# A SwiGLU block's last product: operands combined on chip, or made beforehand in DRAM

## The chip, the core and the metric

One core of one Trainium2 chip runs the whole program. The metric is the time of one execution on the device in microseconds. The kernel before takes 923.42 us, the median of 3 runs (923.11 to 923.51).

## What is computed

One layer on 1024 rows x 1024 channels in float32: a modulation from the conditioning vector, a pooling mixer (`multiscale_pool`), a residual with a layer norm, a SwiGLU with 2816 hidden channels, and a second residual with a layer norm.

```python
mod_x = s_c @ mod_w[i] + mod_b[i]
sh1, sc1, g1, sh2, sc2, g2 = jnp.split(mod_x[:, None, :], N_MOD, axis=-1)
hx = x * (1.0 + sc1) + sh1
ox, oc = pool_mixer(hx, hc, pool_w[j], pool_scale[j], not last)
x = layer_norm(ALPHA * x + g1 * ox, ln_g[i, 0], ln_b[i, 0])
h = x * (1.0 + sc2) + sh2
gt, up = jnp.split(h @ w_in, 2, axis=-1)
y = (jax.nn.silu(gt) * up) @ w_out
x = layer_norm(ALPHA * x + g2 * y, ln_g[i, 1], ln_b[i, 1])
```

## The kernel before

A float32 product is done as three: each operand is split into a high part in float32r (a cast, on ScalarE) and the low part (source less high part, on VectorE), and TensorE multiplies high by high, high by low and low by high. The splits of the last two parts go through `split`, lines 303 to 305.

**Opening** (to about 300 us). Loads, the modulation vectors, the pooling mixer, the first layer norm, the transposed rows `h`, and the first products of the SwiGLU. The order of its jobs is written out by hand (`ORDER_OF_ISSUE`), and `ENGINE_OF` says which engine does what. GpSimd has few jobs at first: line 548 adds two weighted tiles of mod_w, 363 and 368 fill the bands `ends` and `starts` for the pooling of the second half of the rows, 649 multiplies three row tiles by g1, and 701 and 704 fold weighted tiles of mod_w for the second modulation; a column product on TensorE (723) and small VectorE instructions (730 to 734) make gain and shift from these.

**Middle** (about 300 to 604 us). A loop over the tiles f of 128 hidden channels, 2 to 21. GpSimd makes sums of weights (1015 to 1024), ScalarE and VectorE split them (1035, 1041), TensorE does 60 matmuls a tile (1048), VectorE makes the activations a from the banks (1058 to 1080), and SP stores them to DRAM (`a_out`, 1083). The scheduler sets the order of issue here, each engine works in its own order.

**Last product** (about 604 us to the end). y = a @ ffn_w_out in Winograd's form: seven products, each over the 11 pairs of hidden tiles, of half the rows by half the channels. The operands are sums and differences of blocks. They are made on the way: each product has a class with `load`, `combine`, `parts` and `after`; loads bring blocks of a and of ffn_w_out, `combine` and `after` add and subtract them on VectorE and GpSimd (lines 1225, 1253, 1318), `parts` names what is split. `run_ahead` keeps loads, combinations and splits some steps before the matmuls of `sub_pass` (1377), which also carries the jobs of the residual (by_line, 1398; add_into, 1457) and of the last layer norm. Blocks of ffn_w_out are loaded again for each product that uses them.

All DMAs are issued by SP, in order. Each waits for the landing of the one issued eight before it.

Of the kernel before, what the change touches and what calls it, by code (L numbers as in the profile page):

```python
# [256 lines left out]
def trunk_kernel(ctx: ExitStack, tc: tile.TileContext, x, c, mod_w, mod_b, ln_g, ln_b, ffn_w_in, ffn_w_out,  # L257
# [172 lines left out]
    def pool_span(half, g, n):  # L430
        """Input tile n of a half for width g: its columns of the half's bank, cut to what is not zero, the operand."""
# [80 lines left out]
    def mod_col(j, key, first, last):  # L512
        """Partial sums of chunk j as a column, channels on the partitions."""
# [16 lines left out]
    def mod_row(j, *parts):  # L530
        """Chunk j on every partition, in two banks."""
# [47 lines left out]
    def pooled(half, p, h):  # L579
        """256 x 2 columns of the rows at place p of a half through pool_w."""  # L580
# [40 lines left out]
    def scale_bank(h):  # L621
        """pool_scale on every partition."""
# [83 lines left out]
    def mod2_whole(q):  # L706
        """SC2's sum over the partitions as well, on the tensor engine."""
# [73 lines left out]
    a_of = [dram.tile([P, 2, 2, HALF], F32, tag=f"a{pair}", name=f"ad{pair}", bufs=1) for pair in range(NF // 2)]  # L781
# [88 lines left out]
    def pooled_weighed(p):  # L870
        """The shift adds (row sums) x (shift @ pool_w) where the operator's rows do not sum to zero."""
# [730 lines left out]
```

## Time and profile before

| | |
|---|---|
| median of 3 runs | 923.42 us |
| span of the profiled execution | 922.6 us |
| TensorE busy | 780.4 us (85%) |
| VectorE busy | 705.6 us (76%) |
| GpSimd busy | 468.6 us (51%) |
| ScalarE busy | 295.5 us (32%) |
| DMA | 159.81 MB, 173 GB/s on average |

The runs are whole executions; the span is that of one profiled execution, from the first to the last instruction, and lies 0.8 us below the median. PE is TensorE, DVE VectorE, ACT ScalarE, POOL GpSimd, SP the engine that issues DMAs. Matmuls overlap, so busy time of TensorE is no measure of its pace; the number of matmuls in a stretch is.

### The profile page before, as it was taken

Reading aid. Unit: us, or ns where it says so; the run is one execution under the profiler, and the core shown is the slowest. Engines: PE = TensorE matmul, PEld = TensorE weight load, DVE = VectorE, ACT = ScalarE, POOL = GpSimd, SP = SyncE. Lnnn points to the kernel's source line nnn. Section 1 sums busy time; section 2 is a strip of 40 time slices with the busy share of each in tenths; the row PEclk is TensorE's granted clock in tenths of the full one; section 3 lists DMA queues with packets and bytes.
Section 4 is the critical chain, followed back from the end, with each engine's and each line's share of the span. In section 5 each row is a group of like instructions: output and inputs, shape, how many; then the busy total and the mean of one; then the engine's idle time right before and its main releaser. Section 6 shows DMA issues by size and latency. Waiting matters only on the chain. (4 is left out here: it accounts for less than half of the span.)

```text
span 922.6 us, 9749 instructions
## 1 busy us (share of the span) xinstructions
PE 780.4 (85%) x3370; PEld 625.6 (68%) x3370; DVE 705.6 (76%) x782; ACT 295.5 (32%) x506; POOL 468.6 (51%) x273
## 2 busy tenths in 40 slices
PE   6997677888989999997989999859787978888475
PEld 6986555666868888776867787748565855666354
DVE  3579999995371866476575765586999999999996
ACT  2447446723222221122122222224322423334502
POOL 3148668671422434233243543170857577687695
PEclk8699889999989999999889999979898999999787
DMA  8995184823438544554636353669564746610102
GB/s 315 380 358 181 43 254 139 316 91 114 160 120 267 170 127 117 180 160 139 201 106 192 98 155 131 189 250 333 212 207 171 254 146 206 216 45 1 69 23 91
DMA packets 112726, 159.81 MB, mean 173 GB/s; under 512 B 6715, under 2 KB 73987, under 8 KB 112678
## 3 DMA queue, kind: packets, MB, share of 16 engines
q1 hardware_dynamic: 112678, 159.20, 51.6%
q8 instruction: 26, 0.43, 0.2%
q14 instruction: 22, 0.18, 0.1%
HBM read 127.72 MB, written 31.46 MB: 173 GB/s over the span
## 5 line engine op out<-in xcount | busy, mean ns | idle before, releaser
L1377 PE MATMUL ps_x<-yop,yop 128*128 128x512 f32 (+1 forms) x693 | 174.1, 410 | 49.5 <-DVE yop L305 40.8
L1048 PE MATMUL ps_v<-t,ws 128*128 128x512 f32 x792 | 191.3, 399 | 11.4 <-ACT ws L1035 10.3
L1377 PEld LDWEIGHTS ps_x<-yop,yop 128*128 128x128 f32 x693 | 133.3, 203 | 90.0 <-DVE yop L305 53.8
L1048 PEld LDWEIGHTS ps_v<-t,ws 128*128 128x128 f32 x792 | 151.6, 193 | 48.0 <-ACT ws L1035 12.4
L816 PE MATMUL ps_gate<-h,wih 128*128 128x512 f32 x352 | 119.5, 422 | 13.7 <-DVE wih L798 6.5
L305 DVE TENSOR_TENSOR yop<-ya,yop 128x512 fp32r<-128x512 f32 x101 | 111.6, 1129 | 10.5 <-ACT yop L304 10.4
L1041 DVE TENSOR_TENSOR ws<-s,ws 128x512 fp32r<-128x512 f32 x64 | 54.0, 850 | 80.2 <-ACT ws L1035 79.4
L1015 POOL TENSOR_TENSOR s<-raw,raw 128x512 f32<-128x512 f32 x22 | 31.1, 1411 | 134.7 <-DMA raw<-in_ffn_w_in 87.9
L1398 POOL TENSOR_TENSOR yrow<-yrow,yline 128x1024 f32<-128x1024 f32 (+2 forms) x32 | 77.5, 2431 | 38.0 <-ACT yline L1395 16.1
L816 PEld LDWEIGHTS ps_gate<-h,wih 128*128 128x128 f32 x352 | 71.5, 205 | 31.3 <-ACT gk L827 4.8
L304 ACT CAST yop<-ya 128x512 fp32r<-128x512 f32 x101 | 59.3, 617 | 96.2 <-PE ps_x L1377 61.5
L1035 ACT CAST ws<-s 128x512 fp32r<-128x512 f32 x66 | 40.4, 619 | 149.3 <-DMA ad<-a 40.9
L816 PE MATMUL ps_gate<-h,wil 128*128 128x512 f32 x176 | 74.1, 421 | 8.8 <-DVE wil L803 8.7
L1048 PE MATMUL ps_v<-h,ws 128*128 128x512 f32 x264 | 65.9, 400 | 15.2 <-DVE upb L1063 15.2
L1048 PEld LDWEIGHTS ps_v<-h,ws 128*128 128x128 f32 x264 | 50.5, 193 | 27.6 <-DVE upb L1063 17.2
L1377 PE MATMUL ps_y<-yop,yop 128*128 128x512 f32 x264 | 63.8, 400 | 4.1 <-DVE yop L305 4.0
L1225 POOL TENSOR_TENSOR ya<-ya,ya 128x512 f32<-128x512 f32 x25 | 40.6, 1623 | 49.9 <-DMA yw<-in_ffn_w_out 25.1
L1048 PE MATMUL ps_v<-t,wu 128*128 128x512 f32 x264 | 63.4, 389 | 0.0
L1377 PEld LDWEIGHTS ps_y<-yop,yop 128*128 128x128 f32 x264 | 49.8, 191 | 17.9 <-DVE yop L305 7.6
L1048 PEld LDWEIGHTS ps_v<-t,wu 128*128 128x128 f32 x264 | 49.6, 188 | 10.3
L481 DVE SCALAR_TENSOR_TENSOR acc<-mw,s_col,acc 128x1024 f32<-128x1024 f32 (+1 forms) x30 | 43.5, 1462 | 14.4 <-DMA mw<-in_mod_w 14.0
L1024 POOL TENSOR_TENSOR s<-raw,s 128x512 f32<-128x512 f32 x22 | 32.8, 1492 | 37.5 <-DVE ws L1041 37.5
(202 smaller groups left out, 1306.7 us busy)
## 6 DMA issues: line engine op xcount, KB each, us to landing
raw<-in_ffn_w_in SPq DMA_DIRECT2D x88, 256.0 KB, 4.5
mw<-in_mod_w SPq DMA_DIRECT2D x32, 512.0 KB, 6.6
yw<-in_ffn_w_out SPq DMA_DIRECT2D x56, 256.0 KB, 4.2
wi<-in_ffn_w_in SPq DMA_DIRECT2D x22, 512.0 KB, 5.0
ad<-a SPq DMA_DIRECT2D x22, 512.0 KB, 3.5
ya<-ad SPq DMA_DIRECT2D x22, 512.0 KB, 6.8
m<-in_mod_w SPq DMA_DIRECT2D x16, 512.0 KB, 9.1
yline<-in_ffn_w_out SPq DMA_DIRECT2D x27, 256.0 KB, 3.2
```

What stands on the lines that cost most here:

```text
L304: nc.scalar.copy(hi, src)
L305: nc.vector.tensor_tensor(lo, src, hi.bitcast(F32), ALU.subtract)
L481: nc.vector.scalar_tensor_tensor(acc, w, s_col[:, k : k + 1], acc, ALU.mult, ALU.add)
L816: nc.tensor.matmul(ps, x, y, start=k == n == 0, stop=k % 4 == 3 and n == 2, skip_group_check=k > 3)
L1015: nc.gpsimd.tensor_tensor(s, up1, up2, ALU.add)
L1024: nc.gpsimd.tensor_tensor(s, tiles["raw", f, 1][:, 0], s, ALU.subtract)
L1035: nc.scalar.copy(t[:, 0], source(f, name))
L1041: engine(pick(f"vl.{name}_{f}", "DVE")).tensor_tensor(t[:, 1], source(f, name), t[:, 0].bitcast(F32), ALU.subtract)
L1048: nc.tensor.matmul(ps, x, y, start=fresh and first, stop=last, skip_group_check=not fresh)
L1225: e.tensor_tensor(dst, x, y, ALU.subtract)
L1377: nc.tensor.matmul(ps, s[:, x, r * P : (r + 1) * P], t[:, y, d], start=fresh and j == m == 0, stop=j == PAIRS - 1 and m == 2, skip_group_c ...
L1398: nc.gpsimd.tensor_tensor(res[i][:, s], res[i][:, s], lines[name][:, s], op)
```

## The change

Three things change.

The combinations of ffn_w_out are made once for all pairs, in DRAM, by nine transfers that GpSimd issues (`e_step`): four sums e0 to e3 of blocks, each 128 x 11 x 512. A transfer copies a block, copies a sum, or accumulates a block onto a sum. The loop calls one for each tile from 3 to 11.

The combinations of the activations are made by VectorE in `a_out`, at the second tile of each pair, with four instructions of 128x512; SP stores a11, a2, s12 and s43 for each pair. Signs move to the end: some products are now subtracted from the residual (`take_from`).

The last product then only loads two ready blocks for each step (`step_load`), splits both at once (`step_split`, 128x1024), and multiplies. Additions to the residual go from GpSimd to VectorE, the product with g2 in the last of the seven goes from its weights to its result, and the last norm of the first half of the rows goes from ScalarE and GpSimd to two VectorE instructions a tile.

```diff
+    a11_of, a2_of, s12_of, s43_of = pieces("a11", 1), pieces("a2", 2), pieces("s12", 2), pieces("s43", 2)
+    e_of = [dram.tile([P, NF // 2, HALF], F32, tag=f"e{n}", name=f"ed{n}", bufs=1) for n in range(1, 5)]
...
     def a_out(f):
-        nc.sync.dma_start(a_of[f // 2][:, :, f % 2], tiles["a", f])
+        j, a = f // 2, tiles["a", f]
+        if f % 2 == 0:
+            nc.sync.dma_start(a11_of[j][:, 0], a[:, 0])
+            return
+        nc.sync.dma_start(a2_of[j], a)
+        a21, s12, s43 = tiles["a", f - 1][:, 1], act_tile(f"s12_{j}"), act_tile(f"s43_{j}")
+        s1, s2 = s12[:, 0], s12[:, 1]
+        nc.vector.tensor_tensor(s1, a[:, 1], a21, ALU.subtract)
+        nc.vector.scalar_tensor_tensor(s2, s1, -1.0, tiles["a", f - 1][:, 0], ALU.mult, ALU.subtract)
+        nc.sync.dma_start(s12_of[j], s12)
+        for n in range(2):
+            nc.vector.scalar_tensor_tensor(s43[:, n], a[:, n], -1.0, s2, ALU.mult, ALU.subtract)
+        nc.sync.dma_start(s43_of[j], s43)
...
-    class Product1:
-        def load(j):
...
-    products = (Product1, Product2, Product6, Product5, Product3, Product7, Product4)
...
+    w_out = ffn_w_out.rearrange("(j r p) d -> p r j d", p=P, r=2)
...
+    E_STEPS = [(0, block(0, 1), False), (2, block(0, 1), False), (0, block(0, 0), True), (2, block(1, 1), True),
+               (1, 0, False), (3, 2, False), (1, block(1, 1), True), (3, block(0, 0), True), (3, block(1, 0), True)]
+
+    def e_step(n):
+        dst, src, add = E_STEPS[n]
+        src = e_of[src] if isinstance(src, int) else src
+        nc.gpsimd.dma_start(e_of[dst], src, **({"accum_op": ALU.add} if add else {}))
...
+    PARTS = ((lambda j: a11_of[j][:, 0], lambda j: w_out[:, 0, j, first]),
+             (lambda j: a2_of[j][:, 0], lambda j: w_out[:, 1, j, first]),
+             (lambda j: s12_of[j][:, 1], lambda j: e_of[1][:, j]),
+             (lambda j: s12_of[j][:, 0], lambda j: e_of[0][:, j]),
+             (lambda j: s43_of[j][:, 0], lambda j: w_out[:, 1, j, second]),
+             (lambda j: s43_of[j][:, 1], lambda j: e_of[2][:, j]),
+             (lambda j: a2_of[j][:, 1], lambda j: e_of[3][:, j]))
...
+    def step_load(n):
+        t = raw[n] = big(f"yraw{n}", F32, (P, 2, HALF))
+        for m, part in enumerate(PARTS[n // PAIRS]):
+            nc.sync.dma_start(t[:, m], part(n % PAIRS))
+
+    def step_split(n):
+        hi, lo = (big(f"y{q}{n}", F32R, (P, 2, HALF)) for q in ("hi", "lo"))
+        split(hi, lo, raw.pop(n))
...
+    LOADS, SPLITS = 7, 3
...
     def add_into(i, s, src):
-        nc.gpsimd.tensor_tensor(res[i][:, s], res[i][:, s], src, ALU.add)
+        z = res[i][:, s]
+        nc.vector.tensor_tensor(z, z, src, ALU.add)
...
+    E_AT = PLANNED + 1
...
+        if 0 <= f - E_AT < len(E_STEPS):
+            e_step(f - E_AT)
...
-            jobs.append((r / 2 + 5, lambda i=i: row_norm(i, whole)))
...
+            jobs.append((2 * r + 5, lambda i=i: row_centre(i, whole)))
+            jobs.append((2 * r + 6, lambda i=i: row_scale(i, whole)))
...
-            nc.vector.tensor_tensor(res[i][:, d], ps, res[i][:, d], ALU.add)
+            scaled(c[r][:, d], ps, d)
+            add_into(i, d, c[r][:, d])
```

What each engine is given, in order, shows where the nine transfers come to stand. First GpSimd's program from the fill of the accumulator `acc` on, before; `mw` are tiles of mod_w, `ox` the pooled rows, `g` is g1, `m` tiles of mod_w for the second modulation. In brackets is what a row waits for: DMAHW and DMASW are landings of transfers that SP and GpSimd issued.

```order
L486 MEMSET acc_161 128x1024
L548 TENSOR_TENSOR mw_1_178<-mw_1_178,mw_3_183 128x1024 [waits Activation_49]
L363 TENSOR_SCALAR ends<-consts 128x4x128 [waits DMAHW6_49,DMAHW7_49,DMAHW2_49,DVE_49]
L363 TENSOR_SCALAR ends<-consts 128x4x8 [waits DMAHW1_49]
L368 TENSOR_SCALAR starts<-consts 128x4x8
L368 TENSOR_SCALAR starts<-consts 128x4x120
L548 TENSOR_TENSOR mw_1_300<-mw_1_300,mw_3_278 128x1024 [waits DMAHW2_49,Activation_49]
L649 TENSOR_TENSOR ox_2_456<-ox_2_456,g_89 128x1024 [waits DVE_49]
L649 TENSOR_TENSOR ox_1_415<-ox_1_415,g_89 128x1024
L649 TENSOR_TENSOR ox_0_417<-ox_0_417,g_89 128x1024 [waits Pool_49]
L701 TENSOR_TENSOR m_3_0_0_493<-m_3_0_0_493 128x512 [waits DMAHW7_49,Activation_49]
L701 TENSOR_TENSOR m_3_0_0_493<-m_3_0_0_493 128x256 [waits Pool_49]
```

The same engine in the changed kernel, from the second transfer on (the first stands five rows before). `ed_136` to `ed_139` are the sums e0 to e3; the line numbers of after are some lines further on.

```order
L1200 DMA ed_138<-in_ffn_w_out 1408x1x512
L1200 DMA ed_136<-in_ffn_w_out 1408x1x512 [waits DMASW0_49]
L548 TENSOR_TENSOR mw_1_215<-mw_1_215,mw_3_220 128x1024 [waits Activation_49]
L363 TENSOR_SCALAR ends<-consts 128x4x128 [waits DMAHW6_49,DMAHW7_49,DMAHW2_49,DVE_49]
L1200 DMA ed_138<-in_ffn_w_out 1408x1x512 [waits DMASW1_49]
L1200 DMA ed_137<-ed_136 64x11264 [waits DMASW2_49]
L363 TENSOR_SCALAR ends<-consts 128x4x8 [waits DMAHW1_49]
L368 TENSOR_SCALAR starts<-consts 128x4x8
L368 TENSOR_SCALAR starts<-consts 128x4x120
L1200 DMA ed_139<-ed_138 64x11264 [waits DMASW3_49]
```

All nine stand in the opening, though the loop calls them. Between the jobs of the first modulation stand a copy out of ffn_w_out, two accumulations that wait for the copies, and two copies of sums that wait for the accumulations. GpSimd goes on after them so:

```order
L548 TENSOR_TENSOR mw_1_337<-mw_1_337,mw_3_315 128x1024 [waits DMAHW2_49,Activation_49]
L1200 DMA ed_137<-in_ffn_w_out 1408x1x512 [waits DMASW4_49]
L1200 DMA ed_139<-in_ffn_w_out 1408x1x512 [waits DMASW5_49]
L649 TENSOR_TENSOR ox_2_493<-ox_2_493,g_89 128x1024 [waits DVE_49]
L649 TENSOR_TENSOR ox_1_452<-ox_1_452,g_89 128x1024
L649 TENSOR_TENSOR ox_0_454<-ox_0_454,g_89 128x1024 [waits Pool_49]
L701 TENSOR_TENSOR m_3_0_0_530<-m_3_0_0_530 128x512 [waits DMAHW7_49,Activation_49]
L1200 DMA ed_139<-in_ffn_w_out 1408x1x512 [waits DMASW7_49]
L701 TENSOR_TENSOR m_3_0_0_530<-m_3_0_0_530 128x256 [waits Pool_49]
```

The last accumulation stands between the first and the second fold and waits for the one before it. On VectorE, in the fourth of the seven products, before (`ya`, `yw`, `yline` are blocks, `yop` operands):

```order
L1225 TENSOR_TENSOR ya_4209<-ya_4209 128x512
L305 TENSOR_TENSOR yop_4223<-ya_4219,yop_4223 128x512 [waits PE_49,Activation_49]
L305 TENSOR_TENSOR yop_4224<-ya_4212,yop_4224 128x512 [waits Activation_49]
L1225 TENSOR_TENSOR ya_4210<-ya_4210 128x512
L305 TENSOR_TENSOR yop_4225<-ya_4220,yop_4225 128x512 [waits PE_49,Activation_49]
L305 TENSOR_TENSOR yop_4226<-yline_4239,yop_4226 128x512 [waits Activation_49]
```

And in the changed kernel, in the same product:

```order
L305 TENSOR_TENSOR ylo_5246<-yraw_5156,yhi_5245 128x1024 [waits DMAHW6_49,DMAHW5_49,Activation_49]
L305 TENSOR_TENSOR ylo_5265<-yraw_5177,yhi_5264 128x1024 [waits DMAHW7_49,DMAHW0_49,Activation_49]
L305 TENSOR_TENSOR ylo_5284<-yraw_5198,yhi_5283 128x1024 [waits DMAHW2_49,DMAHW1_49,Activation_49]
L305 TENSOR_TENSOR ylo_5303<-yraw_5219,yhi_5302 128x1024 [waits DMAHW4_49,DMAHW3_49,Activation_49]
L305 TENSOR_TENSOR ylo_5322<-yraw_5242,yhi_5321 128x1024 [waits DMAHW7_49,DMAHW0_49,Activation_49]
```

A step there is one instruction of 1024 in the place of three of 512.

## Rows read from the trace of the kernel before

**Rows 1.** The page: busy tenths of each engine, and of the DMA engines, in 40 equal slices of the span.

```profile
PE   6997677888989999997989999859787978888475
DVE  3579999995371866476575765586999999999996
POOL 3148668671422434233243543170857577687695
DMA  8995184823438544554636353669564746610102
```

**Rows 2.** Instructions that write or read the operands `yop` of the last product: line, engine, operation, count: shortest, median and longest in ns, start of the first and of the last in us.

```profile
L1377 PE MATMUL ps_x<-yop,yop x693: 277/389/796, 621.5 to 912.2; 128*128 128x512 f32 x158, 128*128 128x256 f32 x16
L305 DVE TENSOR_TENSOR yop<-ya,yop x101: 646/685/2904, 588.8 to 895.7; 128x512 fp32r<-128x512 f32 x101
```

**Rows 3.** Stretches of the trace: from and to in us, length, busy us of PE, PEld, DVE, ACT and POOL with their instructions, granted TensorE clock, DMA share, GB/s.

```profile
360.00:400.00 40.00, 39.84 (x175) 32.38 (x174) 22.63 (x31) 6.54 (x11) 12.30 (x9) 1.00 0.49 156
...
620.00:640.00 20.00, 20.00 (x90) 16.58 (x89) 14.71 (x19) 7.38 (x13) 3.30 (x2) 1.00 0.75 268
...
720.00:740.00 20.00, 19.71 (x87) 15.68 (x85) 20.00 (x22) 8.01 (x14) 11.43 (x7) 1.00 0.80 260
740.00:760.00 20.00, 14.24 (x57) 10.43 (x58) 20.00 (x23) 5.55 (x10) 15.24 (x11) 1.00 0.43 144
...
800.00:820.00 20.00, 15.37 (x55) 11.25 (x56) 20.00 (x18) 4.59 (x9) 15.47 (x10) 0.91 0.33 107
...
912.40:922.60 10.20, 0.07 (x1) 0.00 (x0) 6.58 (x13) 1.68 (x3) 4.58 (x5) 0.63 0.34 129
```

**Rows 4.** Groups of instructions from 660 us to the end: busy us, mean ns of one, idle time before them and what ended it.

```profile
L1377 PE MATMUL ps_x<-yop,yop 128*128 128x512 f32 x489 | 133.3, 428 | 35.8 <-DVE yop L305 35.7
L305 DVE TENSOR_TENSOR yop<-ya,yop 128x512 fp32r<-128x512 f32 x88 | 96.8, 1128 | 0.0
L1225 POOL TENSOR_TENSOR ya<-ya,ya 128x512 f32<-128x512 f32 x23 | 37.3, 1620 | 26.8 <-ACT yop L304 11.9 <-DVE ya L1225 7.5 <-DMA yw<-in_ffn_w_out 3.8
L1377 PE MATMUL ps_x<-yop,yop 128*128 128x256 f32 x66 | 9.5, 291 | 8.6 <-DVE yv L1551 8.6
```

**Rows 5.** Stretches of the opening, columns as in rows 3.

```profile
0.00:10.00 10.00, 8.77 (x49) 8.43 (x49) 0.31 (x2) 1.28 (x1) 1.63 (x8) 1.00 0.75 245
10.00:20.00 10.00, 4.12 (x18) 4.15 (x18) 4.96 (x5) 3.88 (x5) 2.31 (x1) 0.69 1.00 371
20.00:30.00 10.00, 8.28 (x45) 7.56 (x44) 6.25 (x9) 1.71 (x4) 4.96 (x5) 0.67 1.05 357
30.00:40.00 10.00, 10.00 (x41) 9.14 (x41) 6.24 (x12) 5.80 (x12) 0.00 (x0) 0.50 1.02 406
40.00:50.00 10.00, 10.00 (x81) 10.00 (x81) 8.06 (x10) 4.90 (x9) 2.40 (x1) 0.94 1.08 358
50.00:60.00 10.00, 10.00 (x49) 6.84 (x48) 5.32 (x7) 5.44 (x12) 1.67 (x1) 0.83 1.09 348
60.00:70.00 10.00, 10.00 (x73) 8.95 (x73) 9.86 (x12) 4.16 (x9) 10.00 (x4) 1.00 1.07 372
70.00:80.00 10.00, 5.69 (x36) 5.50 (x35) 9.89 (x12) 9.75 (x23) 9.69 (x8) 0.83 0.76 283
...
90.00:100.00 10.00, 6.36 (x48) 5.60 (x46) 9.65 (x20) 5.09 (x11) 6.20 (x6) 0.96 0.05 19
```

**Rows 6.** GpSimd in order of time: start and length in us, what it does, in brackets the idle time before and what ended it.

```profile
58.33 9.98 POOL L649 TENSOR_TENSOR ox<-ox,g 128x1024 f32<-128x1024 f32 x3 [13.79 <-DVE g L630]
68.27 6.72 POOL L701 TENSOR_TENSOR m<-m 128x512 f32<-128x512 f32 x4
75.07 0.73 POOL L704 TENSOR_TENSOR m<-m,m 128x256 f32<-128x256 f32 x1
```

**Rows 7.** VectorE in order of time, two rows: a residual sum that takes one of GpSimd's products by g1, and the first instruction on the columns of the second modulation.

```profile
62.91 3.18 DVE L654 SCALAR_TENSOR_TENSOR x<-x,ox 128x1024 f32<-128x1024 f32 x1
...
82.06 0.14 DVE L730 SCALAR_TENSOR_TENSOR sc<-ps_m,cols 128x2 f32<-128x2 f32 x1
```

**Rows 8.** Durations of single kinds: a 1024-wide addition on VectorE (order of time), a 1024-wide pass of ScalarE, and a 512-wide addition from a bank on VectorE (groups).

```profile
51.14 1.23 DVE L552 TENSOR_TENSOR acc<-acc,mw 128x1024 f32<-128x1024 f32 x1
...
L1395 ACT ACTIVATE yline<-yline 128x1024 f32<-128x1024 f32 x2 | 2.1, 1060 | 8.3 <-DMA yline<-in_ln_g 4.7 <-DMA yline<-in_ln_b 3.6
...
L1535 DVE TENSOR_TENSOR c<-ps_x,u 128x512 f32<-128x512 f32 x4 | 2.5, 676 | 0.0
```

**Rows 9.** The middle part: one stretch (columns as in rows 3), a wait in total (us, times, longest) from 300 to 600 us, and a group from 300 to 641 us.

```profile
300.00:604.00 304.00, 287.48 (x1226) 232.35 (x1225) 191.18 (x248) 70.22 (x118) 108.68 (x75) 0.98 0.49 154
...
PE ps_v L1048 <- ACT ws L1035: 10.3, 5, 4.5
...
L1063 DVE TENSOR_TENSOR upb<-ps_v,upb 128x512 f32<-128x512 f32 x21 | 14.5, 688 | 0.5
```

**Rows 10.** DMA issues: what they move, queue, count, KB of one, median us from issue to landing.

```profile
yw<-in_ffn_w_out SPq DMA_DIRECT2D x56, 256.0 KB, 4.2
ad<-a SPq DMA_DIRECT2D x22, 512.0 KB, 3.5
ya<-ad SPq DMA_DIRECT2D x22, 512.0 KB, 6.8
...
out<-yrow SPq DMA_DIRECT2D x5, 256.0 KB, 2.0
```

More of the change, by code (lines that the diff above doesn't have):

```diff
@@ L779, in spill, with pieces @@
                 for pair in range(NF // 2)]
-    a_of = [dram.tile([P, 2, 2, HALF], F32, tag=f"a{pair}", name=f"ad{pair}", bufs=1) for pair in range(NF // 2)]
+    def pieces(name, count):
+        return [dram.tile([P, count, HALF], F32, tag=f"{name}{pair}", name=f"{name}d{pair}", bufs=1)
+                for pair in range(NF // 2)]
+    a11_of, a2_of, s12_of, s43_of = pieces("a11", 1), pieces("a2", 2), pieces("s12", 2), pieces("s43", 2)
+    e_of = [dram.tile([P, NF // 2, HALF], F32, tag=f"e{n}", name=f"ed{n}", bufs=1) for n in range(1, 5)]
     p1_of, gate_of = spill("p"), spill("g")
@@ L1199, in trunk_kernel @@
-    borrowed, closed = set(), set()
-    def lend(hs, back=False):
-        if back:
-            closed.update(map(id, hs))
-            w_free[:] = [h for h in w_free if id(h) not in closed]
-        else:
-            borrowed.update(map(id, hs))
-            w_free.extend(hs)
-    def w_release(h):
-        if id(h) not in closed:
-            w_free.append(h)
-    def hidden_load(half, j):
-        t = a_raw[half, j] = two(a_mem[half * PAIRS + j])
-        nc.sync.dma_start(t, a_of[j][:, half])
@@ L1218, in w_load @@
-    def w_load(key, j, rows, s):
-        t = raw[key, j] = w_free.pop(next(n for n, h in enumerate(w_free) if key != "d" or id(h) not in borrowed))
-        f = 2 * j + rows
-        nc.sync.dma_start(t, ffn_w_out[f * P : (f + 1) * P, s])
-    def less(e, dst, x, y):
-        e.tensor_tensor(dst, x, y, ALU.subtract)
-    def weight(key, j):
-        t = raw.pop((key, j))
-        spent.append(t)
-        return t
-    spent = []
-    class Product1:
-        def load(j):
-            hidden_load(0, j)
-            w_load("b11", j, 0, first)
-        def combine(j):
-            pass
-        def parts(j):
-            return a_raw[0, j][:, 0], weight("b11", j)
@@ L1307, in trunk_kernel @@
-    class Product7:
-        def load(j):
-            pass
-        def combine(j):
-            pass
-        def parts(j):
-            return a_raw[0, j][:, 0], a_raw[0, j][:, 1]
-        def after(j):
-            nc.gpsimd.tensor_tensor(raw["d", j], raw["d", j], g2[:, first], ALU.mult)
-            op_free.append(two(place("big", y_place[f"ya{j}"], f"yop{OPS + j}", F32R, (P, 1024))))
-    class Product4:
-        def load(j):
-            pass
-        def combine(j):
-            pass
-        def parts(j):
-            return a_raw[1, j][:, 1], weight("d", j)
@@ L1331, in trunk_kernel @@
-    products = (Product1, Product2, Product6, Product5, Product3, Product7, Product4)
-    steps = [(q, j) for q in range(7) for j in range(PAIRS)]
-    done = {"load": 0, "combine": 0, "parts": 0}
-    def split_parts(q, j):
-        pair = []
-        for n, src in enumerate(products[q].parts(j)):
-            t = op_free.pop(0)
-            split(t[:, 0], t[:, 1], src)
-            pair.append(t)
-        operands[q, j] = pair
-    def advance(kind, upto):
-        while done[kind] < min(upto, len(steps)):
-            q, j = steps[done[kind]]
-            if kind == "load" and len(w_free) < 4 and q > 1:
-                break
-            split_parts(q, j) if kind == "parts" else getattr(products[q], kind)(j)
-            if kind == "parts" and hasattr(products[q], "after"):
-                products[q].after(j)
-            while spent:
-                w_release(spent.pop(0))
+    w_out = ffn_w_out.rearrange("(j r p) d -> p r j d", p=P, r=2)
@@ new lines, in trunk_kernel @@
+    done = {"load": 0, "split": 0}
+    def step_load(n):
[5 more added lines that the diff above has]
+        split(hi, lo, raw.pop(n))
+        operands[n] = hi, lo
+        done_with("big", f"yraw{n}")
+    def advance(kind, upto):
+        while done[kind] < min(upto, STEPS):
+            {"load": step_load, "split": step_split}[kind](done[kind])
@@ L1353, in advance @@
             done[kind] += 1
+    LOADS, SPLITS = 7, 3
     def run_ahead(step):
         advance("load", step + LOADS)
-        advance("combine", step + COMBINES)
-        advance("parts", step + SPLITS)
-        while len(op_free) >= 8 and done["parts"] < min(step + 6, len(steps)):
-            advance("parts", done["parts"] + 1)
+        advance("split", step + SPLITS)
     def sub_pass(q, banks, fresh, heads, tails, jobs=()):
@@ L1507, in trunk_kernel @@
     second_products(NF - 1)
-    done_with("half", f"both{NF - 1}", f"upb{NF - 1}")
-    done_with("bank", f"ps_v{NF - 1}_5", f"ps_v{NF - 1}_7")
+    f = NF - 1
+    done_with("big", f"ws4_{f}", f"wu2_{f}", f"gate_{f // 2}", f"p1_{f // 2}", f"a_{f - 1}", f"a_{f}",
+              f"s12_{f // 2}", f"s43_{f // 2}")
+    done_with("big", *(name for name in LASTING["big"] if name[:2] in ("t4", "h1")))
+    done_with("half", f"both{f}", f"upb{f}")
+    done_with("bank", f"ps_v{f}_5", f"ps_v{f}_7")
     run_ahead(0)
@@ L1552, in trunk_kernel @@
         for r, i in enumerate(ORDER[1]):
-            for n, (s, src) in enumerate(((second, v[r]), (first, u[r]))):
+            for n, (s, src, into) in enumerate(((second, v[r], take_from), (first, u[r], add_into))):
                 more.append((r + n / 2, lambda s=s, src=src: scaled(src, src, s)))
-                more.append((r + n / 2 + 1, lambda i=i, s=s, src=src: add_into(i, s, src)))
+                more.append((r + n / 2 + 1, lambda i=i, s=s, src=src, into=into: into(i, s, src)))
             more.append((r + 3, lambda i=i: row_stats(i, 1, second)))
```

124 lines of the change are left out of this document (27 added, 97 removed).

## Prediction, before the changed kernel was run

> **What bounds the kernel now.** I read the page's slices first, then stretches of the last part, then groups and waits there, and last the opening, because the new transfers stand there in the order of issue. The slices show VectorE at nine tenths from slice 27 to the end, with TensorE below it, and the DMA engines full in the first three slices and never again [rows 1]. So two places count: the last product, and the opening.
>
> The last product runs from its first matmul at 621.5 us to the end at 922.6, so 301 us [rows 2]. TensorE at full pace issues 90 matmuls in 20 us, 0.222 us each, in the stretch from 620 on; from 740 and from 800 it issues 57 and 55 while VectorE is busy for all 20.00 us [rows 3]. VectorE bounds it, and TensorE's longest wait there is for VectorE's split [rows 4]. A split of 128x512 takes 1.13 us on average, though an undisturbed one takes 0.69 (the median), because GpSimd's combinations of 1.6 us each run beside it [rows 2, 4].
>
> In the opening the DMA share is 1.00 to 1.09 from 10 to 70 us, at 348 to 406 GB/s [rows 5]. GpSimd, idle for 13.79 us before it, starts the products by g1 at 58.33 as soon as VectorE has made g1, and VectorE's residual sums follow these [rows 6, 7].
>
> **Last product: the gain.** All combinations leave it (VectorE's and GpSimd's lines 1225 and 1253, GpSimd's 1318), and 154 splits of 512 become 77 of 1024. Nothing of it is left on GpSimd but the residual's lines. What remains:
> - TensorE: 891 matmuls of 512 x 0.222 = 198.0, and 66 half-width ones, 9.5 us busy [rows 3, 4]: 207.5 us.
> - VectorE: 77 splits x 1.23, the undisturbed 128x1024 subtraction or addition [rows 8], = 95 us. Evacuations, products with g2, additions now on VectorE, statistics: about 80 instructions of 0.68 [rows 8] = 54; eight 1024-wide norm steps x 1.23 = 10. Sum 159, below 207.5.
> - ScalarE: 77 casts x 1.06 [rows 8] = 82.
> - Loads: 154 of 256 KB = 40.4 MB in 207.5 us, 195 GB/s; 720 to 740 already moves 260 [rows 3].
>
> So TensorE becomes the bound. It won't be perfect: from 360 to 400 it issues 175 of a possible 180 [rows 3], so I put 207.5 / 0.972 = 213.5. Add 7 us for the starts of seven products (1 us each, an estimate: one bank's evacuation of 0.68 and a handoff [rows 8]), the tail of 10.2 us after the last matmul [rows 3] and 0.7 for the extra product with g2 in it: 231. Gain 301 - 231 = **70 us**. Bounds: 76 at full pace, 50 if TensorE keeps only the pace of the middle part, 1226 x 0.222 = 272 of 304 us [rows 9].
>
> **Middle part: four more VectorE instructions for each pair.** 11 x 4 x 0.69 [rows 9] = 30 us on VectorE, which is busy for 191 of 304 us. They stand ahead of the next tiles' splits, as the order shows, and behind those waits ScalarE, GpSimd's next sum and TensorE. TensorE waits for a split or cast at 5 of the 20 tiles now [rows 9], so I take a quarter: **8 us**; bounds 0 and 30. The two further stores to a pair on SP's queue hold back the loads behind them by the same instructions, and are in these bounds.
>
> **The nine DRAM transfers: the loss.** The loop calls them at tiles 3 to 11, but they read only a kernel input, and the order of issue puts them at the head of GpSimd's program. Call them A to I in that order: A, B copies out of ffn_w_out, C, D accumulations, E, F copies of one sum into another, G, H, I accumulations; each writes 1408 x 512 x 4 = 2.88 MB. C waits for A, D for B, E for C, F for D, G for E, H for F, I for H. GpSimd is in order, so behind E's wait stand the bands `ends` and `starts`, behind F's the sum for g1, behind H's three products by g1, and behind I's wait, which is H's landing, all folds of the second modulation.
>
> Who waits for that: VectorE's residual sums wait for the products, and its columns at 82.06 need the first folds, which GpSimd did from 68.27 to 75.8 [rows 6, 7]. VectorE is in order too and is busy for 9.86 and 9.89 us of the two stretches from 60 to 80 [rows 5]. So the opening ends later by what delays the second fold, at 70.0 now, less some 3 us between the fold's columns and VectorE's arrival.
>
> The price of a transfer isn't in this trace, where nothing is copied from DRAM to DRAM or accumulated. The nearest row is a load under a full DMA: 357 GB/s [rows 5], 2.88 MB in 8.1 us. I take **8 us for a copy** and, as an accumulation must read its target as well, **16 us for an accumulation**. Below, 7.1 us for either (406 GB/s). Above, from 512 KB rows that include their latency [rows 10]: a store to DRAM 3.5 us, so 19 us for 2.88 MB, and a load from a spill 6.8 us, so 37 for an accumulation. The descriptor work on GpSimd I put at nothing: it lies beside the transfers it feeds; without that cover it is unpriced here, and the upper bound has to hold it.
>
> The Trainium skill (Collectives: The Full Stack, "The bandwidth ceiling: the fold count and why AG ≠ RS ≠ AR") says that an adding transfer runs at half a copy's rate because it needs two source reads; no run here shows it yet. The same skill (DMA: Bandwidth & Descriptors, "Latency and other measured facts") has copies between HBM tensors at about 207 GB/s, with longer rows than these; by that a copy is an estimated 14 us and an accumulation 28, and the kernel would take 1033 us.
>
> Until I can be issued, A to H must have landed: 4 x 8 + 4 x 16 = 96 us of all DMA engines. In the same time the opening's own loads up to 70 us must come, 70.6 us of all engines (the shares of the first seven stretches [rows 5]), and the engines are full, so the two add: 167. I add 6 us for three handoffs in which a chain's next transfer isn't yet moving, at 2.0 us, the shortest landing [rows 10]. GpSimd's second fold starts at 173 instead of 70; less 3: **100 us later**. Bounds: 8 x 7.1 + 70.6 - 73 = 54; and 4 x 19 + 4 x 37 + 70.6 - 73 = 222. Little of it comes back: from 90 to 100 the DMA is nearly idle, but VectorE is busy for 9.65 of 10 us [rows 5].
>
> **Sum**, against the profiled execution: 922.6 + 100 + 8 - 70 = 960.6. The runs' median, 923.42, is 0.8 above its span, so 961.4: **961 us, slower**.
>
> **Rivals.**
> 1. *The transfers pass beside the loads.* If the full share comes from the side of on-chip memory, a DRAM to DRAM transfer may not add to it. For it: the engines are idle around 95 [rows 5]. Then A to H, two chains of 8 to 16 us, land by about 75, the delay is 0 to 5, and the time 923.4 + 8 - 70 = 861. Against it: packets of a kind that already fill every engine's time.
> 2. *An accumulation costs no more than a copy.* 8 x 8 + 70.6 + 6 - 73 = 68, so 929; with both lower bounds (54, gain 76, middle 0) 901. This straddles the time before.
> 3. *Accumulations are dear, or their descriptors are*: up to 222 us, so 1083. For it: small pieces of 2 KB, and a wait before each. It shows as GpSimd held for over 200 us.
> 4. *The wait moves inside the last product*: TensorE then waits for loads instead of VectorE, and only half the gain is left, 996. Against it: eight loads are in flight and land in about 4 us [rows 10], seven steps are loaded ahead.
> That the change doesn't do what it says is in part certain: the loop doesn't spread the transfers.
>
> **Chances.** Forecast and what lies near it, with rival 4 (935 to 1000): 0.45. Rival 3 (over 1000): 0.25. Rival 2 (900 to 935): 0.17. Rival 1 (under 900): 0.13. The slow side decides once the delay of GpSimd exceeds 62 us. A range from 885 to 1060 leaves out about half of rival 1 and a third to a half of rival 3; the forecast's own is 935 to 1000. Faster by over 0.2% (about what a measurement can tell from no change): rival 1 and half of rival 2, 0.21; within 0.2%: 0.02; slower: 0.77.
>
> **What would show it.** GpSimd's second fold near 170; DMA share at 1 well past 100 us and more bytes written early; g1's products late by 50 to 80. In the last product, TensorE at 85 or more matmuls in 20 us, VectorE at 7 to 8 tenths, splits at 1.2 to 1.3 us. If the fold stands near 75, rival 1 holds and I am wrong on the sign; if near 140, rival 2.

## The result: half a per cent slower

The changed kernel takes 927.6 us (median of 6 runs, 925.17 to 928.83), the kernel before 923.26 us (6 runs, three of them timed beside it): a ratio of 1.005, interval 1.0034 to 1.0066. The sign was forecast, the size was not: +38 us predicted, about +4 measured.

The page of the changed kernel, busy tenths in 40 slices, answers to [rows 1]:

```profile
PE   4563565777788989899999999999659999999964
DVE  1232452899995381468678777788695764458987
POOL 2212235577662340334253426433445300000005
DMA  9999999974823437266476654746459857571612
```

The DMA engines stand at nine tenths for eight slices of 23 us, where before one stood at eight tenths and two at nine; VectorE stands at one to five tenths in the first six, and in most of the last ten TensorE is at nine tenths and VectorE below it. So both effects that the prediction named are there. Three places cut the time into parts: the last product for the gate on TensorE (the opening's end) in the kernel before, then in the changed one, and the first and last matmul of the changed kernel's last product, which answers to [rows 2]:

```profile
282.81 0.39 PE L816 MATMUL ps_gate<-h,wil 128*128 128x512 f32 x1
```

```profile
359.68 0.39 PE L823 MATMUL ps_gate<-h,wil 128*128 128x512 f32 x1
...
L1250 PE MATMUL ps_x<-yhi x231: 277/389/628, 690.6 to 912.9; 128*128 128x512 f32 x105, 128*128 128x256 f32 x11
```

| part | before, us | after, us | measured | forecast |
|---|---|---|---|---|
| opening, to the last product for the gate | 282.8 | 359.7 | +76.9 | +100 |
| middle, to the first matmul of the last product | 338.7 | 330.9 | -7.8 | +8 |
| last product, to the end of the span | 301.1 | 235.9 | -65.2 | -70 |
| span | 922.6 | 926.5 | +3.9 | +38 |

The opening is where the loss is. GpSimd in order of time (answers to [rows 6]); L1200 are the transfers, here C, D, E and F, and I in the row before the last:

```profile
18.89 1.76 POOL L1200 DMA_DIRECT2D ed<-in_ffn_w_out  x1 [13.98 <-DMA ed<-in_ffn_w_out]
33.96 1.80 POOL L1200 DMA_DIRECT2D ed<-in_ffn_w_out  x1
54.45 0.55 POOL L1200 DMA_DIRECT2D ed<-ed  x1 [18.69 <-DMA ed<-in_ffn_w_out]
80.11 0.56 POOL L1200 DMA_DIRECT2D ed<-ed  x1 [22.14 <-DMA ed<-in_ffn_w_out]
...
111.37 9.95 POOL L649 TENSOR_TENSOR ox<-ox,g 128x1024 f32<-128x1024 f32 x3 [11.77 <-DVE g L630]
...
137.77 2.03 POOL L1200 DMA_DIRECT2D ed<-in_ffn_w_out  x1 [14.94 <-DMA ed<-in_ffn_w_out]
138.67 3.91 POOL L701 TENSOR_TENSOR m<-m 128x256 f32<-128x256 f32 x3
```

The products by g1 come 53 us later than in [rows 6]. The second fold starts at 138.67; the prediction had it at 173. Below, what each queue of DMAs had done in the first 138 us: packets, MB, time of its packets as a share of 16 engines. q0 carries GpSimd's transfers, q1 what SP issues.

```profile
q0 software_dynamic: 7296, 23.07, 67.4%
q1 hardware_dynamic: 8516, 17.44, 37.6%
```

In 138 us the transfers A to H took 0.674 x 138 = 93 us of all engines; the prediction's price was 96. The loads took 52 us, and not the 70.6 that had been needed to get there in [rows 5]. That is the main difference, and it is taken up below. The engines stay full behind it (columns as in [rows 3]; the last three are clock, DMA share and GB/s):

```profile
80.00:110.00 30.00, 13.22 (x34) 8.46 (x35) 6.28 (x6) 3.32 (x6) 6.41 (x4) 0.56 1.02 290
...
140.00:180.00 40.00, 25.59 (x158) 23.16 (x157) 20.63 (x43) 20.12 (x43) 20.13 (x20) 0.77 1.09 310
```

Behind the fold it is the loads that come late. [rows 7] has VectorE's first columns of the second modulation at 82.06; now they come at 146.84, 65 us later. The next ones come at 172.36, 77 us later (95.52 before), since ScalarE waits for a load of mod_w in between:

```profile
163.57 0.51 ACT L696 ACTIVATE m<-m,s_col 128x256 f32<-128x256 f32 x1 [13.29 <-DMA m<-in_mod_w]
...
172.36 0.15 DVE L730 SCALAR_TENSOR_TENSOR sc<-ps_m,cols 128x2 f32<-128x2 f32 x1
```

In the last product TensorE is now the bound until about 870 us, and VectorE again near the end:

```profile
740.00:760.00 20.00, 20.00 (x90) 16.57 (x89) 11.48 (x14) 4.22 (x4) 0.00 (x0) 1.00 0.58 189
...
860.00:880.00 20.00, 20.00 (x98) 16.86 (x97) 20.00 (x23) 6.94 (x7) 0.00 (x0) 1.00 0.70 236
880.00:900.00 20.00, 12.81 (x44) 8.51 (x43) 18.69 (x26) 1.05 (x1) 0.00 (x0) 0.72 0.16 53
```

### The profile page after: what moved, and what is told of

Its sections match the earlier page's. It is cut to its first block, busy times and chain, and to the rows that moved or that the text cites. A ratio compares the mean times of both kernels' runs of the same rounds, so it can differ in the third digit from the quotient of the medians.

```text
span 926.5 us, 9471 instructions
## 1 busy us (share of the span) xinstructions
PE 770.6 (83%) x3370; PEld 631.3 (68%) x3370; DVE 612.0 (66%) x724; ACT 282.2 (30%) x425; POOL 314.9 (34%) x191
## 3 DMA queue, kind: packets, MB, share of 16 engines
q0 software_dynamic: 8720, 25.95, 11.7%
## 4 chain that ended last, share of the span: by engine, by line
PE 33%; DVE 26%; DMA 17%; issue 8%; SPq 8%; POOL 4%; ACT 2%; POOLq 0%; DVEq 0%; ACTq 0%
PE ps_v L1055 14%; PE ps_x L1250 14%; DMA mw<-in_mod_w 5%; SPq L332 5%; PE ps_y L1250 3%; DVE acc L481 3%; DMA m<-in_mod_w 3%; DVE ws L1048 3%; SPq L387 2%; PE ps_gate L823 2%; DMA halo<-in_x 2%; DVE wil L810 2%; DMA raw<-in_ffn_w_in 2%; DVE ylo L305 1%; DMA wi<-in_ffn_w_in 1%
## 5 line engine op out<-in xcount | busy, mean ns | idle before, releaser
L304 ACT CAST yhi<-yraw 128x1024 fp32r<-128x1024 f32 x77 | 78.1, 1050 | 118.0 <-DMA yraw<-in_ffn_w_out 38.1
L305 DVE TENSOR_TENSOR ylo<-yraw,yhi 128x1024 fp32r<-128x1024 f32 x77 | 99.2, 1327 | 13.5 <-ACT yhi L304 13.5
L1272 POOL TENSOR_TENSOR yrow<-yrow,line_lg 128x1024 f32<-128x1024 f32 (+2 forms) x12 | 26.7, 2229 | 222.5 <-ACT yrow L1303 183.2
L1250 PE MATMUL ps_x<-ylo,yhi 128*128 128x512 f32 (+1 forms) x231 | 90.0, 390 | 7.2 <-DVE ylo L305 7.0
L1250 PE MATMUL ps_x<-yhi 128*128 128x512 f32 (+1 forms) x231 | 89.0, 385 | 0.0
L1250 PE MATMUL ps_x<-yhi,ylo 128*128 128x512 f32 (+1 forms) x231 | 89.0, 385 | 0.0
L1048 DVE TENSOR_TENSOR ws<-s,ws 128x512 fp32r<-128x512 f32 x64 | 58.0, 910 | 43.6 <-ACT ws L1042 42.7
L1027 POOL TENSOR_TENSOR s<-s,raw 128x512 f32<-128x512 f32 x22 | 33.0, 1501 | 86.8 <-DVE ws L1048 86.7
L1250 PEld LDWEIGHTS ps_x<-ylo,yhi 128*128 128x128 f32 x231 | 44.3, 192 | 18.5 <-DVE ylo L305 10.2
L1250 PEld LDWEIGHTS ps_x<-yhi 128*128 128x128 f32 x231 | 44.3, 192 | 8.6
```

The source lines that it names most:

```text
L304: nc.scalar.copy(hi, src)
L305: nc.vector.tensor_tensor(lo, src, hi.bitcast(F32), ALU.subtract)
L1027: nc.gpsimd.tensor_tensor(s, s, tiles["raw", f, 0][:, 0], ALU.subtract)
L1048: engine(pick(f"vl.{name}_{f}", "DVE")).tensor_tensor(t[:, 1], source(f, name), t[:, 0].bitcast(F32), ALU.subtract)
L1250: nc.tensor.matmul(ps, s[x][:, r * P : (r + 1) * P], t[y][:, d], start=fresh and j == m == 0, stop=j == PAIRS - 1 and m == 2, skip_group_c ...
L1272: nc.gpsimd.tensor_tensor(res[i][:, s], res[i][:, s], lines[name][:, s], op)
```

## Experiments

Parts are measured as above; e1, without transfers, is the base line for the others: 280.9, 330.4 and 235.5 us. Openings with the same instructions lasted 277.9 (e2) to 284.3 us (e9), so differences of some 3 us in an opening say nothing.

**What the transfers cost (e1), and at what price (e3, e4).**

```diff
-        if 0 <= f - E_AT < len(E_STEPS):
-            e_step(f - E_AT)
...
-             (lambda j: s12_of[j][:, 1], lambda j: e_of[1][:, j]),
+             (lambda j: s12_of[j][:, 1], lambda j: w_out[:, 0, j, second]),
```

> The changed kernel without its nine transfers; the last product loads plain blocks of ffn_w_out where it loaded the sums e0 to e3 (same sizes), so its result lacks those sums. If the opening's delay comes from the transfers alone, the last product starts 77 us earlier than in the changed kernel, near 614 us, and the time is 927.6 - 77 = 851 us. Rival: the 8 us that the middle part gained were a consequence of the late opening (weights lying ready); then the middle takes its former 338 us and the time is about 859 us.

Measured: 849.4 us, ratio 0.919 (0.916 to 0.923). The opening is back, and the middle still takes 330.4 us: so its gain doesn't come from the late opening.

```diff
-        nc.gpsimd.dma_start(e_of[dst], src, **({"accum_op": ALU.add} if add else {}))
+        nc.gpsimd.dma_start(e_of[dst], src)
```

> The changed kernel with the five accumulations made plain copies (same blocks, same chains of waits; the sums are missing from the result). Theory, an accumulation costs twice a copy: 4 x 7.75 + 5 x 15.5 = 108 us, what the nine took of all DMA engines; nine copies then take 70 us, the opening is late by about 0.71 x 70 = 50 instead of 77, and the time is 900 us. Rival, copy and accumulation cost the same 12 us: GpSimd's queue again takes 108 us of all engines, and the time stays at 927 us.

Measured: 897.3 us, ratio 0.971 (0.967 to 0.975). GpSimd's queue on the page of the changed kernel, and of this one:

```profile
q0 software_dynamic: 8720, 25.95, 11.7%
```

```profile
q0 software_dynamic: 5200, 25.95, 7.7%
```

Same bytes, 108.4 us of all engines (0.117 x 926.5) against 68.9 (0.077 x 894.2). So a copy costs 7.65 us and an accumulation (108.4 - 4 x 7.65) / 5 = 15.6, a factor of 2.0, and each accumulation has 704 more packets ((8720 - 5200) / 5). The prediction's 8 and 16 were right; rival 2 falls. The Trainium skill (Collectives: The Full Stack, "The bandwidth ceiling: the fold count and why AG ≠ RS ≠ AR") gives the half rate for the adding step of a collective. The trace agrees, here for a plain accumulation on one core (15.6 us against 7.65). The Trainium skill's 207 GB/s for copies between HBM tensors (DMA: Bandwidth & Descriptors, "Latency and other measured facts"), measured there with longer rows, is not what these cost: 2.88 MB in 7.65 us of all engines is 377 GB/s.

For e4 the copies go into nine tensors of their own, from inputs, so that none waits for another:

```diff
-        src = e_of[src] if isinstance(src, int) else src
-        nc.gpsimd.dma_start(e_of[dst], src)
+        src = ffn_w_in[:P].rearrange("p (j d) -> p j d", d=HALF) if n in (4, 5) else src
+        nc.gpsimd.dma_start(apart[n], src)
```

> Nine plain copies of the same sizes and row lengths, each into a tensor of its own from a kernel input, so that no transfer waits for another and GpSimd is not held (only the ninth waits, for the first); the result lacks the sums. Against the copies with their chains: if the delay comes from sharing the DMA engines, it is the same within 10 us, about 900 us. If it comes from GpSimd standing in front of each wait, it goes almost wholly, and the time is 855 to 865 us.

Measured: 898.5 us, ratio 0.972 (0.969 to 0.976), the same as with the chains. The opening ends 50 us after that of e1, with chains 46. The second fold comes 5 us earlier than with chains (105.55 against 110.22), and that doesn't help. So GpSimd's waits, on which the prediction built its path, cost nothing of their own beside copies; beside accumulations no run takes them away. What delays the opening is that its loads share the engines.

**Transfers where the loop means them (e2, e5).** Each is queued behind the tile's last sum on GpSimd.

```diff
+            with tc.issue_after(last_sum[f].ins):
+                e_step(f - E_AT)
```

> The changed kernel with each of the nine transfers queued on GpSimd behind the tile's last sum of weights, so that they stand at tiles 3 to 11 of the loop. The middle part's DMA share was 0.47 to 0.63 and the transfers take 108 us of all engines in some 160 us. If idle DMA time hides them, the opening is as before, the middle loses up to 10 us to later weights, and the time is 851 to 861 us. Rival: beside the transfers every load of weights lands in 20 us instead of 5, as the loads of the opening did, and GpSimd stops at each chain's wait; then TensorE waits in nine tiles for some 5 us each and more, and the time is 890 us or more.

Measured: 918.3 us, ratio 0.996 (0.993 to 0.999). The rival's time came true, but not its loads of 20 us: a load of weights landed in 5.3 us (median). The opening is whole again, and the middle takes 397.7 us, 67 more than in e1.

> As with the transfers at tiles 3 to 11, but one at every second tile, 3, 5, ... 19. Theory: what cost 67 us there was too much for the DMA engines at once: nine tiles last 150 us, of which the loop's own loads and stores take half, and the transfers want 108. In eighteen tiles, 300 us, 150 are free for 108. Then the middle takes 330 to 345 us and the time is 849 to 865 us. Rival: a load of weights that meets a transfer is late whatever the mean share is, because they split the engines; each of the nine transfers then stops TensorE about as before, 4 to 7 us each, and the time is 885 to 915 us.

Measured: 917.8 us, ratio 0.993 (0.991 to 0.996); the middle takes 399.3 us. Spreading changes nothing, so the theory of too many at once fell. Median landing in e5's middle, and in the middle of e1:

```profile
raw<-in_ffn_w_in SPq DMA_DIRECT2D x72, 256.0 KB, 7.3
...
s43d<-s SPq DMA_DIRECT2D x9, 512.0 KB, 11.6
```

```profile
raw<-in_ffn_w_in SPq DMA_DIRECT2D x72, 256.0 KB, 4.7
```

A load of weights takes 7.3 us instead of 4.7 (19.2 at most), and TensorE waits for what is made of it, as in two stretches of e5 and a wait in total:

```profile
443.00:463.00 20.00, 19.12 (x74) 14.97 (x75) 12.78 (x16) 4.85 (x9) 8.72 (x7) 0.90 0.99 278
463.00:483.00 20.00, 14.92 (x57) 11.49 (x56) 12.74 (x18) 3.52 (x6) 4.43 (x5) 0.87 0.89 294
...
PE ps_v L1057 <- ACT ws L1044: 39.5, 8, 9.2
```

**Smaller pieces, more lead (e9, e11, e12).** e9 cuts each transfer into eleven; e11 is e5 with `weights_load(f + 3)` for `weights_load(f + 2)`; e12 is both.

```diff
-        nc.gpsimd.dma_start(e_of[dst], src, **({"accum_op": ALU.add} if add else {}))
+        nc.gpsimd.dma_start(e_of[dst][:, j], src[:, j], **({"accum_op": ALU.add} if add else {}))
```

> The nine transfers cut into eleven pieces each, one for each pair of hidden tiles (99 of 256 KB, the same rows and bytes), pipelined over tiles 3 to 21 behind the sums of weights on GpSimd. Theory: a long transfer is dear because the loads beside it land late for some 20 us on end; pieces of 0.7 and 1.4 us delay a load little, so the middle falls from 399 us to 335 to 355 and the time to 855 to 875 us. Rival: only the total of DMA time counts (0.6 us for each of the 108), the middle stays at 390 to 400 us and the time at 915 us or more, more still if GpSimd's 99 issues and waits hold back its sums.

> The transfers whole, one at every second tile as in the run with the 399 us middle, and the weights loaded three tiles ahead instead of two. Theory: TensorE stops there because the loads that meet a transfer land up to 19 us after issue instead of 5; a tile more of lead (16 us) covers most of it, the middle falls to 335 to 360 us and the time to 855 to 880 us. Rival: what the transfers take is TensorE's feed in another way (stores and spilled sums that come late too); then the middle stays above 385 us and the time above 903 us.

> Both: 99 pieces over tiles 3 to 21, and weights three tiles ahead. If pieces and lead each take away part of the delay, the middle is 330 to 345 us and the time 849 to 865 us, the best of all. Rival: GpSimd's issues and waits for pieces hold its sums of weights however early the weights land; then it is no better than the pieces alone.

| | time, us | ratio (interval) | middle, us |
|---|---|---|---|
| e9 | 914.6 | 0.988 (0.985 to 0.992) | 391.3 |
| e11 | 909.5 | 0.982 (0.979 to 0.986) | 389.6 |
| e12 | 898.6 | 0.972 (0.967 to 0.976) | 375.7 |

All three missed what was hoped of them. Each takes away 8 to 24 of the 69 us; in the middle part neither length nor lead is the whole cause. The traces show in part what keeps the other 45. First, the rival of e9 and e12 came true: GpSimd's 99 issues keep it busy for 72 us of e12's middle (busy us, count, clock, DMA share, GB/s), and it waits for pieces ahead of its sums (us, times, longest):

```profile
280.00:656.00 376.00, 72.39 (x99) 0.92 0.86 238
...
POOL ed L1202 <- DMA ed<-in_ffn_w_out: 21.9, 12, 4.8
```

Second, so did that of e11: the stores land late too. ScalarE's casts of weights, for which TensorE waits, themselves wait for stores of the sums, 69 us in e11 and 20 in e1:

```profile
ACT ws L1044 <- DMA s12d<-s: 40.3, 3, 16.6
ACT ws L1044 <- DMA s43d<-s: 29.1, 3, 14.8
```

Third, a wait of TensorE costs more than its own length. TensorE in the middles of e1 and e5, then twice 2 us of e5 (busy us, count, granted clock, DMA share, GB/s):

```profile
280.90:611.30 330.40, 306.73 (x1326) 0.96 0.59 190
```

```profile
282.81:682.10 399.29, 326.93 (x1326) 0.91 0.78 223
...
475.00:477.00 2.00, 0.00 (x0) 1.00 0.46 184
...
481.00:483.00 2.00, 2.00 (x6) 0.50 1.02 281
```

Of the 69 us, 49 are idle time of TensorE, and 20 are the same matmuls taking longer. After the idle stretch around 476 us the granted clock is 0.50, the lower of its two levels (1.2 GHz), and TensorE issues 6 matmuls in 2 us, where 90 in 20 us is its pace at 1.00. How the 45 us divide between these three isn't shown.

**The middle's own gain (e7, e8, e10).** e7 stores the activations of two tiles together in the kernel before; e8 is e1 without the sums; e10 is the kernel before with weights loaded three tiles ahead.

```diff
-        nc.sync.dma_start(a_of[f // 2][:, :, f % 2], tiles["a", f])
+        if f < 20 and f % 2 == 0:
+            return
+        for n in (f - 1, f) if f < 20 else (f,):
+            nc.sync.dma_start(a_of[n // 2][:, :, n % 2], tiles["a", n])
```

> The kernel before with one change in the loop: the activations of an even tile are stored together with those of the next tile (up to tile 19), so that SP's queue stands at a store once in two tiles. Theory: the middle part of the changed kernel is 8 us shorter because fewer loads of weights stand behind a store that waits for its activations; then the middle takes 330 to 334 us instead of 338.5 and the time is 915 to 919 us. Rival: the gain lies in something else (the loop's other order, memory places); then the time stays within 2 us of the kernel before.

```diff
-        nc.vector.tensor_tensor(s1, a[:, 1], a21, ALU.subtract)
...
-        nc.sync.dma_start(s12_of[j], s12)
+        nc.sync.dma_start(s12_of[j], tiles["a", f - 1])
```

> The changed kernel without transfers, and also without the 44 sums of activations on VectorE: the stores to s12 and s43 take the activations themselves, in the same places and sizes, so its result lacks the sums. Theory: the sums lie beside TensorE, and leaving them out gains 0 to 2 us: 847 to 850 us. Rival, the prediction's term: a quarter of their 30 us is on TensorE's path, so about 841 us.

```diff
+    weights_load(PLANNED + 2)
...
-        if f + 2 < NF:
-            weights_load(f + 2)
+        if f + 3 < NF:
+            weights_load(f + 3)
```

> The kernel before, with the weights of a tile loaded three tiles ahead instead of two, nothing else. Theory: the middle part's length goes with how long GpSimd waits for loads of weights (33 us of waiting with 330 us, 88 with 338.5, 98 with 343.7, 136 with 343.4); loaded earlier, the middle takes 330 to 334 us and the time is 914 to 919 us. Rival: it is the order of VectorE or something else that the sums changed; then the wait shrinks and the time stays within 2 us of the kernel before.

Measured: e7 929.3 us, ratio 1.006 (1.004 to 1.008); e8 861.5, 0.931 (0.928 to 0.935), so 12 more than e1 with 44 instructions fewer; e10 913.3, 0.988 (0.984 to 0.992). Both theories on e8 fell, and that on pairing too (e7 also holds the even tile's place in memory for one tile longer). GpSimd's wait for loads of weights in the middle, in us, times and longest, of the kernel before, the changed one, e7, e8 and e10:

```profile
POOL s L1015 <- DMA raw<-in_ffn_w_in: 87.9, 9, 27.5
```

```profile
POOL s L1022 <- DMA raw<-in_ffn_w_in: 33.6, 6, 12.3
```

```profile
POOL s L1015 <- DMA raw<-in_ffn_w_in: 135.8, 13, 36.4
```

```profile
POOL s L1022 <- DMA raw<-in_ffn_w_in: 98.2, 11, 35.8
```

```profile
POOL s L1015 <- DMA raw<-in_ffn_w_in: 38.7, 2, 33.6
```

The middles are 338.7, 330.9, 343.4, 343.7 and 331.5 us: those with 34 to 39 us of waiting take 331, those with 88 to 136 take 339 to 344. e10 asks for nothing but earlier loads, and goes from one group to the other. That the changed stores led to an order of SP in which the weights come sooner is argued; e7 shows only that pairing alone doesn't do it.

**By place (e6, e13, e14).** e6 queues seven transfers in the opening by the DMA share, two in the loop.

> The same nine transfers placed by the profile: seven queued on GpSimd in the opening where its DMA share was 0.01 to 0.6 (two copies at about 75 us, an accumulation at 95, one at 180, the two copies of sums at 205 and 228, an accumulation at 239), the last two at tiles 6 and 10 of the loop. If it is the DMA engines' time and nothing else, five to seven of them cost nothing and the last two 0 to 7 us each: 849 to 863 us. Rival: GpSimd's work of issuing, or a shared path beyond the engines' time, still costs; then 870 us or more.

Measured: 899.7 us, ratio 0.973 (0.969 to 0.977): an opening 29 us longer than e1's, a middle 22 longer. One of the transfers tells more than the mean. GpSimd in e6, and the same two jobs in e1:

```profile
182.06 2.83 POOL L963 TENSOR_TENSOR d<-h,h 128x1024 f32<-128x1024 f32 x1 [3.24 <-issue]
...
249.33 2.10 POOL L1206 DMA_DIRECT2D ed<-in_ffn_w_out  x1
265.75 2.35 POOL L814 TENSOR_TENSOR wil<-wi,wih 128x1024 fp32r<-128x1024 f32 x1 [14.32 <-DVE wih L809]
```

```profile
179.44 2.82 POOL L959 TENSOR_TENSOR d<-h,h 128x1024 f32<-128x1024 f32 x1 [3.25 <-issue]
...
240.20 2.39 POOL L810 TENSOR_TENSOR wil<-wi,wih 128x1024 fp32r<-128x1024 f32 x1 [1.19 <-DVE wih L805]
```

After three transfers (31 us of all engines) at 75 to 100 us, the job at 179 is 2.6 us late, which is within the spread of openings. The accumulation issued at 249 makes the next gate weights late, and GpSimd's next job stands at 265.75 instead of 240.20, where it had been 10 late before (247.04 for 236.62): one accumulation cost 15 us, its whole price. So e13 looks for gaps only:

```diff
+    for n, name, k in ((0, "fold", 0), (1, "fold", 0), (2, "hlo", 0), (4, "vl", 0), (6, "td", 0)):
+        with tc.issue_after(marks[name][k]):
+            e_step(n)
...
+    def e_behind(n, t):
+        nc.gpsimd.tensor_scalar(turn, t[:, :1], 1.0, None, ALU.mult)
+        e_step(n)
```

> All nine transfers, by place: two copies and an accumulation at 75 to 100 us, the copy for e1 at about 142, its accumulation at about 182 us (DMA share 0.03 and 0.1 there without transfers), and the other four one by one in the last product, on GpSimd behind tiny instructions that read a result of the product before. Theory, the place decides: the middle is as without transfers, 330 us, the opening 3 to 10 us later, the last product 235 to 250 us, so the time is 852 to 872 us, against 849 without transfers. Rival, the total of DMA time decides, at 0.4 to 0.6 us for each of its 108: 892 to 914 us.

> The same, and the weights of the middle part loaded three tiles ahead instead of two. That took 7 us off the middle of the kernel before, where GpSimd's wait for loads fell from 88 to 39 us; here GpSimd waits only some 33 us for them, and TensorE at 5 us or less beside the wait at the end of the loop. So 0 to 3 us less than without it: 850 to 872 us. Rival: the lead helps any middle by 7 us.

Measured: e13 852.0 us, ratio 0.923 (0.920 to 0.927); e14 851.0, 0.921 (0.918 to 0.924). e13 is 2.6 us above e1, with all nine transfers (13.3% of the span on the page, 113 us of all engines): parts of 281.4, 331.4 and 235.9 us. Two stretches of e1, then of e13:

```profile
80.00:110.00 30.00, 21.52 (x132) 18.19 (x131) 29.26 (x52) 16.30 (x30) 18.37 (x17) 0.94 0.12 36
...
700.00:720.00 20.00, 20.00 (x90) 16.57 (x89) 16.84 (x18) 7.39 (x7) 0.00 (x0) 1.00 0.91 300
```

```profile
80.00:110.00 30.00, 22.44 (x125) 18.65 (x124) 29.32 (x47) 14.28 (x25) 20.58 (x17) 0.89 1.00 263
...
700.00:720.00 20.00, 20.00 (x90) 16.55 (x89) 17.52 (x19) 8.36 (x8) 1.96 (x2) 1.00 1.06 253
```

In the gap the share goes from 0.12 to 1.00 and VectorE stays busy. In the last product the engines are full and TensorE issues its 90 matmuls all the same; that seven steps of loads are under way there is the likely reason. The place decides, not the total of DMA time. The lead of e14 adds nothing beyond the noise; in e13 GpSimd waited for weights for only 17.3 us.

## Why the prediction was right in its sign and wrong in its size

The sum came out at +3.9 us, less than any of the three parts was off (23, 16 and 5 us). That the sign is right is therefore luck in part.

**Last product: right.** TensorE became the bound. The chain of waits holds 264 matmuls in one piece, and only one wait for a load of operands (start, us), so rival 4 falls:

```profile
690.72 59.84 PE ps_x L1250 x264
...
872.22 4.73 DMA yraw<-ed
```

It took 235.9 us instead of 231: that load comes late, the statistics and norm steps of the first half keep VectorE busy for 20.00 and 18.69 of 20 us from 860 on, with 44 matmuls in the second of these stretches, and from the end of the last matmul to the end it is 13.1 us instead of 10.9. I had counted VectorE's work over the whole part and not where it stands.

**Place and price of the transfers: right.** They stand at the head of GpSimd's program, and A to H took 93 us where 96 were forecast.

**Opening: the step that failed is "the engines are full, so the two add: 167".** It let all 70.6 us of the opening's loads land before I is issued. At 138 us the loads had had 52, beside the 93 of the transfers, together 145 us of engine time in 138 us (the share is above one). I waits for the transfers alone, and the loads don't go first. The two queues stand level by packets, here from 40 to 50 us, and from 80 to 90, where a sum is copied in long rows (packets, MB, share of 16 engines):

```profile
q0 software_dynamic: 727, 1.49, 80.0%
q1 hardware_dynamic: 732, 0.88, 30.5%
...
q0 software_dynamic: 90, 3.33, 93.4%
q1 hardware_dynamic: 88, 0.33, 11.5%
```

The Trainium skill (DMA: Bandwidth & Descriptors, "Queues, rings and completion order") says that an engine serves its queues in turn, a packet of each; the trace agrees. The time isn't level, as the transfers' packets take longer: from 80 to 90 the loads got 1.2 of 10 us.

The second fold came 69 us late instead of 103 (100 after the 3 us that I took off). Of the 34 us between, 19 are the loads that were still due, 7 the share above one, 6 the handoffs, which didn't show, and 3 the price. Another 8 were lost behind the fold, since the loads then still due kept the engines full to 180 us and ScalarE waited for one of them (the row at 163.57). So the path was wrong as well: the opening's end follows its loads, and not the second fold alone. I had also named the wrong holder, GpSimd's waits, which e4 takes away without gain, though with copies only. Of the 31 us by which the delay stays below the transfers' 108, an estimated 26 can be put down to engine time that e1 leaves idle from 80 to 110 us (0.88 x 30). I had seen that gap and let little come back, since VectorE was busy there; but it is the transfers that use it, as e13 shows.

**Middle: the step that failed is the quarter of 30 us.** I priced the four sums and not the order that comes with the change: 8 us gained instead of lost, probably through earlier weights (e10).

**Rivals.** 1 (beside the loads) falls: e3 and e4 lose 46 and 50 us to 69 us of copies. 2 and 3 fall by the price. The time landed in the range of rival 2, and so did its sign (the fold near 140, measured 138.67), for another reason: an accumulation does cost two copies.

**A reading.** In [rows 1] VectorE stands at nine tenths from slice 29 to 39, and not from 27 to the end; nothing was added up from it.

## What to carry to other kernels

Price a transfer from DRAM to DRAM by the time that it takes of all DMA engines, an accumulation at two copies, and then ask not what the mean DMA share is but which loads run beside it and how soon they are needed: beside loads needed at once it cost up to its whole price, in a gap or beside loads with seven steps of lead next to nothing (2.6 us for all nine in e13). A DMA that depends on no instruction isn't placed by the loop that calls it; it has to be tied to an instruction that stands where the trace has its gap. Where two queues fill the engines, count what the waiting instruction needs, not all that is under way, and expect the queue with the longer packets to get more of the time.

## What wasn't expected of the hardware

That a part with full DMA engines (shares of 0.97 to 1.12 in e13 from 620 to 760 us) loses no matmul, while in the middle a share of 0.78 on the mean (e5, 283 to 660 us: 47.3% and 31.1% of the two queues) cost 69 us, and one tile more of lead gave back only 10 of them. Why the middle is so much more sensitive is shown only in part: its loads and stores land later, GpSimd's issues take its time where the transfers are cut up, and the granted clock falls after TensorE's waits.
